# Both recurrence gates of 128 channels in the four quarters of the TensorE array, the second gate from a copy of its input with the halves exchanged

## The chip, the cores and the metric

The kernel runs on one core of one Trainium2 chip. The metric is the time of one execution on the device in microseconds (us); the number that counts is the median of a few runs. A profile is one further execution, recorded by the hardware profiler.

A core has five engines with a queue each: PE (TensorE: matmuls; the loads of their stationary operand are shown apart, as PEld), DVE (VectorE), ACT (ScalarE), POOL (GpSimd) and SP (SyncE, which in this kernel issues all DMA transfers). Each engine works through its queue in the order of the program; an instruction that has to wait holds up all that stand behind it.

## What is computed

Two layers over 256 context and 256 latent tokens of width 1024. Each layer is a half feed-forward block, a token mixer with four branches, and a second half feed-forward block. One of the four branches is a recurrence (RG-LRU) over 256 channels, in both directions; the change touches its two gates alone. Cut to them:

```
LRU_BLOCKS = 4                       # 256 channels in 4 blocks of 64
def rglru_coeffs(u, w_a, b_a, w_x, b_x, lam):
    ub = u.reshape(b, t, LRU_BLOCKS, w // LRU_BLOCKS)
    r = sigmoid(einsum('btnc,nce->btne', ub, w_a).reshape(b, t, w) + b_a)
    i = sigmoid(einsum('btnc,nce->btne', ub, w_x).reshape(b, t, w) + b_x)
    log_a = -LRU_C * r * softplus(-lam)
    return exp(log_a), sqrt(-expm1(2.0 * log_a)) * (i * u)
def rglru_mixer(...):
    u = dw_conv(xr, lru_conv_w, LRU_CONV_K // 2) + lru_conv_b
    for direction, reverse in ((0, False), (1, True)):
        a, b = rglru_coeffs(u, ...)
        h = linear_scan(a, b, h0, reverse)
```

So each gate multiplies every block of 64 channels by a 64x64 matrix of its own, for 512 tokens, and there are two gates, two directions, four blocks and two layers.

## The kernel before, in words

All activations lie with channels on partitions and tokens in columns. The large products (L196, three passes in a reduced format that stand for one full-precision product) make up nearly all of the kernel; their weights come in by DMA (L128), three buffers deep, and are split into a high and a low part by ACT (L150) and DVE (L151).

In the mixer, `self.recurrence` is a generator whose pieces are put between the large products by a clock of planned time (`later`, `spend`; a `yield n` asks for the next piece n planned nanoseconds later). A scheduler of the framework then sets the final order on each engine; that order is fixed before the run. Two attention branches are woven in by the same clock (`attend`): scores (L721, two heads at a time, each on 64 partitions), transposes of the probabilities (`turn`, L701, into the PSUM bank `C`), and values (L735, two heads at a time, each into 64 columns of the array). `heads` uses the bank `E` for small transposes (`flip`, L638). PSUM tiles have a tag each, with so many buffers: `A` 3, `B` 2, `C` 1, `D` 1, `E` 1.

The recurrence takes 128 channels (`c`, two of them) and a direction (`d`) at a time, so four steps in a layer and eight in the kernel. `U[c]` holds the 128 channels of its input for both halves of the tokens; it comes out of four DVE operations (`conv`, L569 and three of L575). For each gate `gate` runs two fp32 matmuls of 128x128 by 256 columns (L772) with a block-diagonal stationary operand `bd`: two 64x64 matrices on the diagonal, zeros beside them. Both write the bank `E`, and ACT takes it from there with a Tanh (L773). The second gate follows 1300 planned ns after the first. `bd` is loaded once for a layer.

An fp32 matmul stands in the trace as two records. Counts of "x4" and the like below are records.

Of the kernel before, what the change touches and what calls it, by code (L numbers as in the profile page):

```python
# [8 lines left out]
F32 = mybir.dt.float32  # L9
F32R = mybir.dt.float32r  # L10
AF = mybir.ActivationFunctionType
# [4 lines left out]
L = 2  # L16
# [19 lines left out]
class Net:  # L36
# [13 lines left out]
        self.n += 1  # L50
        return f"{s}{self.n}"

    BUFS = dict(b=12, nb=2, nr=2, ya=4, yp=4, m=8, a=6, l=5, r=3, t=2)
    BANKS = dict(A=3, B=2, C=1, D=1, E=1)

    def blk(self, tag, shape=(128, 512), dt=F32):
# [264 lines left out]

    def first_factors(self, n, s, R):
        nc = self.nc
        ms = self.small((64, 128), "ms", 2)
        nc.vector.tensor_scalar(ms, n["ps"][s], 1.0 / D, EPS, op0=ALU.mult, op1=ALU.add)
        pt = self.ps("A", (128, 2, 32))
        nc.tensor.transpose(pt[:].rearrange("p g n -> p (g n)"), ms, self.ident[:64, :64])
        v = self.small((128, 2), "v4")
        nc.vector.tensor_copy(v, pt[:, :, 0])
        for f in self.factors(n, s, v, R):  # L330
            f()
# [425 lines left out]
                T[b, 1] = self.turn(P.pop(b)[1], nk(b))  # L757
            yield 2 * step

    def recurrence(self, segs, out, U, bd, sp2, hb, step):  # L760
        nc = self.nc
        S3 = lambda x: x[:].rearrange("p (s t) -> p s t", s=2)
        for c in range(2):
            for d in range(2):
                k = 2 * d + c
                u = U[c] if d == 0 else U[c][:, ::-1, :]

                def gate(j, g):
                    pz = self.ps("E")
                    for s in range(2):  # L770
                        src = s if d == 0 else 1 - s
                        nc.tensor.matmul(pz[:, 256 * s:256 * s + 256], bd[:, 4 * j + k], U[c][:, src], start=True, stop=True)  # L772
                    nc.scalar.activation(g, pz, AF.Tanh, scale=0.5, bias=hb[:, 4 * j + k:4 * j + k + 1])  # L773

                t, q, b = (self.blk("r") for _ in range(3))
                gate(0, t)
                yield 1300
                gate(1, b)
                nc.scalar.activation(q, t, AF.Exp, scale=sp2[:, 4 + k:5 + k], bias=sp2[:, 4 + k:5 + k])
                nc.scalar.activation(t, t, AF.Tanh, scale=sp2[:, k:k + 1], bias=sp2[:, k:k + 1])  # L780
                nc.vector.scalar_tensor_tensor(S3(b), S3(b), 1.0, u, op0=ALU.add, op1=ALU.mult)
                yield step
                w = self.blk("t")
                nc.vector.tensor_scalar(q, q, 1.0, None, op0=ALU.add)
                nc.vector.scalar_tensor_tensor(w, t, 1.0, q, op0=ALU.add, op1=ALU.mult)
                nc.vector.scalar_tensor_tensor(q, w, 4.0, q, op0=ALU.subtract, op1=ALU.mult)
                nc.scalar.activation(t, t, AF.Sqrt)
                nc.vector.tensor_tensor(t, t, q, op=ALU.mult)
                nc.vector.tensor_scalar(q, q, -0.5, -1.0, op0=ALU.mult, op1=ALU.add)
                nc.vector.tensor_tensor(b, b, t, op=ALU.mult)  # L790
                h = self.blk("ya") if d == 0 else t
                w = slice(None) if d == 0 else slice(None, None, -1)
                nc.vector.tensor_tensor_scan(h[:, w], q[:, w], b[:, w], 0.0, op0=ALU.mult, op1=ALU.add)
                if d == 0:
                    f = h
                yield step
            for s in segs:
                w, w2 = slice(256 * s, 256 * s + 256), slice(256 * (1 - s), 256 * (1 - s) + 256)
                nc.vector.tensor_tensor(f[:, w], f[:, w], h[:, w2], op=ALU.add)
            out.append(f)  # L800

    def mixer(self, l, H, nxt):
# [4 lines left out]
        lo, hi = qr  # L807
        segs = self.segs(qr)
        ns = len(segs)
        bd = self.sp.tile([128, 8, 128], F32, name=self.nm("bd"), tag="bd", bufs=1)  # L810
        nc.sync.dma_start(bd, self.a["bd"][l])
        sp2, hb = self.softplus_terms(l)
        gq = self.head_gains(l)
# [8 lines left out]


        two = lambda: self.blk("b", (128, 2, 256))
        U, dk, dv = [two(), two()], [two(), two()], [two(), two()]
        wf, wt = self.take("fm", l, 0), self.take("tm", l, 0)
        F = [self.ps("A"), self.ps("A")]
# [14 lines left out]
        for c in range(2):  # L842
            t = self.blk("m", (128, 2, 256))
            nc.scalar.activation(t, F[c][:].rearrange("p (s t) -> p s t", s=2), AF.Copy)
            self.conv(U[c], t, lambda k: par[:, O_LW + 2 * k + c:O_LW + 2 * k + c + 1], [(0, 2), (-2, 0), (-1, 1), (1, 3)],
                      par[:, O_LB + c:O_LB + c + 1])

        gain = lambda j: gq[:, 64 * j:64 * j + 64]
        Y = [None, [], [], []]
        self.later(5000, lambda: self.job(self.recurrence(segs, Y[2], U, bd, sp2, hb, 5500 if full else 7000), (l, "lru")))  # L850
        dq = [two() if full else None, two()]
        self.tokens(l, 1, H, qr, lambda t, ps: self.heads(ps, t, 4, gain(2), dq, None, "m"))
        self.tokens(l, 2, H, ALL, lambda t, ps: nc.scalar.activation(dv[t // 2][:, t % 2], ps, AF.Copy))
# [160 lines left out]
def layout(x, c, ctx, c_ctx, w_mod, b_mod, norm_g, ffn_w_gate, ffn_w_up, ffn_w_down, w_in, b_gate, conv_a_w,  # L1014
           qk_norm_g, attn_sink, lru_conv_w, lru_conv_b, lru_w_a, lru_b_a, lru_w_x, lru_b_x, lru_lam, na_rel_bias,
           w_branch, w_out):
    A = {}
    t = np.concatenate([ctx[0], x[0]], axis=0)
    A["x"] = t.T.reshape(KC, 128, NT)
    A["c"] = np.stack([c_ctx, c[0]], axis=1).reshape(KC, 128, 2).transpose(1, 0, 2)  # L1020
    A["cst"] = constants()
    sets = []
    for i in range(3):
        sets += [[24 * i + 2 * s, 24 * i + 2 * s + 1, 24 * i + 8 + 2 * s, 24 * i + 9 + 2 * s] for s in range(4)]
        sets += [[24 * i + 16 + 4 * s + g for g in range(4)] for s in range(2)]
    sets = np.array(sets)
    wm = w_mod.reshape(L, 2, 4, 128, 72, 128)[:, :, :, :, sets]
    A["first"] = wm[0, :, :, :, :4].transpose(3, 0, 2, 1, 4, 5).reshape(4, 2, 128, 2048)
    A["mod"] = w_mod.reshape(L, D, 72, 128)[:, :, sets].transpose(0, 2, 3, 4, 1).reshape(L, 18, 2, 2, 128, D) \
        .transpose(0, 1, 2, 4, 3, 5).reshape(L, 18, 2, 128, 2048)  # L1030
    A["rows"] = np.broadcast_to(np.stack([c_ctx, c[0]]).reshape(1, 2, 2, 512), (128, 2, 2, 512))
    gu = np.stack([ffn_w_gate, ffn_w_up], axis=2).reshape(L, 2, 2, KC, 128, FT, 128)
    A["gu"] = gu.transpose(0, 1, 5, 4, 2, 3, 6).reshape(L, 2, FT, 128, 2048)
    dn = ffn_w_down.reshape(L, 2, 2, FH, 128, 8, 128)
    A["dn"] = dn.transpose(0, 1, 2, 5, 4, 3, 6).reshape(L, 2, 2, 8, 128, FH * 128)
    part = lambda n, w: w_in[:, :, COL[n]:COL[n] + w]
    fm = np.stack([part(n, 256) for n in FM], axis=1).reshape(L, 5, KC, 128, 2, 128)
    A["fm"] = fm.transpose(0, 1, 3, 4, 2, 5).reshape(L, 5, 128, 2048)
    tmw = np.stack([part(n, 256) for n in TM], axis=1)
    perm = np.concatenate([np.arange(64 * h, 64 * h + 64) for pr in HEADS for h in pr])  # L1040
    tmw[:, 4] = tmw[:, 4][:, :, perm]
    A["tm"] = tmw.reshape(L, 5, KC, 128, 256).transpose(0, 1, 3, 2, 4).reshape(L, 5, 128, 2048)
    gl = w_in[:, :, COL["gl"]:].reshape(L, KC, 128, 4, 8, 128).transpose(0, 3, 4, 2, 1, 5)
    wb = np.array(w_branch)
    wb[:, 1] = wb[:, 1][:, perm]
    wb = wb.reshape(L, 4, 2, 128, 8, 128).transpose(0, 1, 4, 3, 2, 5)
    A["gb"] = np.concatenate([gl, wb], axis=4).reshape(L, 4, 8, 128, 1280)
    wo = w_out.reshape(L, KC, 128, 4, 2, 128)
    A["wo"] = wo.transpose(0, 3, 2, 4, 1, 5).reshape(L, 4, 128, 2048)
    col = lambda v: v.reshape(L, -1, 128).transpose(0, 2, 1)  # L1050
    bm = b_mod.reshape(L, 72, 128)[:, sets.reshape(-1)]
    par = [col(norm_g), bm.transpose(0, 2, 1), col(b_gate), col(conv_a_w), col(lru_conv_w), col(lru_conv_b),
           col(lru_b_a), col(lru_b_x), col(lru_lam)]
    A["par"] = np.concatenate(par, axis=2)
    rep = np.concatenate([qk_norm_g.reshape(L, 256), attn_sink], axis=1)
    A["rep"] = np.broadcast_to(rep[:, None, :], (L, 128, 260))
    bd = np.zeros((L, 2, 2, 2, 2, 64, 2, 64), np.float32)
    for j, w in enumerate((lru_w_a, lru_w_x)):
        w = w.reshape(L, 2, 2, 2, 64, 64)
        for b in range(2):  # L1060
            bd[:, j, :, :, b, :, b, :] = w[:, :, :, b]
    A["bd"] = bd.reshape(L, 8, 128, 128).transpose(0, 2, 1, 3)
    A["nb"] = na_rel_bias[:, :, :, ::-1]
    return {k: np.ascontiguousarray(v) for k, v in A.items()}

# [23 lines left out]
```

## Time and profile before

| | |
|---|---|
| median of 3 runs | 2020.85 us (2020.05 to 2020.87) |
| time of the profiled execution | 2021.12 us |
| its span, first to last instruction | 2019.2 us |
| PE / PEld / DVE / ACT / POOL busy | 99% / 86% / 66% / 40% / 5% |
| granted TensorE clock | 1.000 (2.4 GHz) over the span |
| DMA | 295.50 MB, 146 GB/s on average |

Engine busy shares are averages over stages. The time of an execution is its span and about 2 us around it; the profiled execution is 0.27 us above the median. A piece of the chain of waits reads: start in us, length in us, what was done, and how many records it holds.

### The profile page before, as it was taken

To read this page: it belongs to the slowest core of one execution; us is meant where nothing else is said; L and a number is where in the kernel's file an instruction comes from. 1 tells how busy PE (TensorE), PEld (TensorE's weight loads), DVE (VectorE), ACT (ScalarE), POOL (GpSimd) and SP (SyncE) were. 2 spreads that over 40 slices of the span, in tenths; PEclk is the share of its full clock that TensorE was granted. 3 is DMA by queue.
4 is the path that set the end of the run, shared out by engine and by line. 5 is a ranking of instruction groups with operands and counts; after the bars stand their busy time and mean duration, and the time that the engine had idled before them with its cause. 6 is when DMAs were issued, how large, how long until landed. Compare 5 with 4: busy or idle time off the path is not lost.

```text
span 2019.2 us, 29778 instructions
## 1 busy us (share of the span) xinstructions
PE 1997.5 (99%) x11732; PEld 1732.6 (86%) x11732; DVE 1329.5 (66%) x2905; ACT 799.8 (40%) x1311; POOL 102.5 (5%) x105
## 2 busy tenths in 40 slices
PE   7999999999999999999999999999999999999999
PEld 5888887897797788988888898888888999999999
DVE  5869986677455545685733368689844788775554
ACT  4322222366334434332223233322323676664443
POOL 0000000220010000200000020000002101010000
PEclk9999999999999999999999999999999999999999
DMA  9645653522221234253522234446434224463553
GB/s 351 212 175 194 222 191 133 175 69 67 80 87 66 79 102 149 84 183 138 190 104 92 72 140 157 163 170 245 178 123 138 82 92 139 152 232 146 174 186 122
DMA packets 61548, 295.50 MB, mean 146 GB/s; under 512 B 14688, under 2 KB 16352, under 8 KB 38240
## 3 DMA queue, kind: packets, MB, share of 16 engines
q1 hardware_dynamic: 61408, 293.60, 41.7%
q8 instruction: 92, 1.51, 0.3%
q14 instruction: 48, 0.39, 0.1%
HBM read 292.53 MB, written 1.05 MB: 145 GB/s over the span
## 4 chain that ended last, share of the span: by engine, by line
PE 93%; DVE 3%; DMA 2%; issue 1%; ACT 1%; POOL 0%; SPq 0%; ACTq 0%; POOLq 0%; DVEq 0%
PE A L196 56%; PE B L196 32%; DVE a L256 1%; DMA b<-in_first 1%; PE B L721 1%; PE D L735 1%; PE C L701 1%; DVE wl L151 1%; PE E L772 1%; DMA w<-in_dn 0%; DMA par<-in_par 0%; PE E L638 0%; DMA yp<-in_first 0%; ACT wh L150 0%; DVE x L452 0%
## 5 line engine op out<-in xcount | busy, mean ns | idle before, releaser
L150 ACT ACTIVATE wh<-w 128x1024 fp32r<-128x1024 f32 (+2 forms) x476 | 428.2, 905 | 863.9 <-PE A L196 364.4
L196 PE MATMUL A<-h,wh 128*128 128x512 f32 (+1 forms) x2880 | 750.3, 348 | 1.3 <-DVE h L393 0.7
L151 DVE TENSOR_TENSOR wl<-w,wh 128x1024 fp32r<-128x1024 f32 (+2 forms) x476 | 490.3, 1033 | 287.4 <-ACT wh L150 284.8
L196 PEld LDWEIGHTS A<-h,wh 128*128 128x128 f32 x2880 | 496.6, 189 | 73.5 <-issue 10.9
L196 PE MATMUL A<-h,wl 128*128 128x512 f32 (+1 forms) x1440 | 494.9, 344 | 1.6 <-DVE wl L151 1.6
L196 PE MATMUL B<-h,wh 128*128 128x512 f32 (+1 forms) x1472 | 397.5, 355 | 0.0
L256 DVE CUSTOM_DVE_ANT_0 a<-w,rows 128x512 f32<-128x512 f32 x512 | 351.5, 697 | 35.8 <-DMA w<-in_mod 26.7
L196 PEld LDWEIGHTS A<-h,wl 128*128 128x128 f32 x1440 | 272.6, 189 | 35.3 <-DVE wl L151 2.9
L196 PEld LDWEIGHTS B<-h,wh 128*128 128x128 f32 x1472 | 261.8, 189 | 38.7
L196 PE MATMUL B<-h,wl 128*128 128x512 f32 (+1 forms) x736 | 261.1, 355 | 0.2 <-DVE wl L151 0.2
L196 PEld LDWEIGHTS B<-h,wl 128*128 128x128 f32 x736 | 139.1, 189 | 20.0 <-DVE wl L151 0.6
L354 POOL TENSOR_TENSOR nb<-nb,l 128x256 f32<-128x256 f32 x60 | 60.6, 1023 | 1360.2 <-ACT l L352 1360.2
L196 PE MATMUL A<-b,wh 128*128 128x512 f32 (+1 forms) x492 | 126.3, 346 | 1.8 <-ACT wh L150 1.8
L485 DVE TENSOR_TENSOR t<-t,B 128x512 f32<-128x512 f32 (+1 forms) x88 | 54.2, 618 | 106.5 <-PE B L196 105.5
L196 PE MATMUL B<-b,wh 128*128 128x512 f32 (+1 forms) x408 | 110.7, 358 | 0.0
L196 PEld LDWEIGHTS A<-b,wh 128*128 128x128 f32 x492 | 85.9, 189 | 13.9 <-ACT wh L150 2.7
L196 PE MATMUL A<-b,wl 128*128 128x512 f32 (+1 forms) x246 | 85.1, 346 | 0.8 <-DVE wl L151 0.8
L196 PE MATMUL A<-wh,h 128*128 128x256 f32 x448 | 84.9, 287 | 0.0
L196 PEld LDWEIGHTS B<-b,wh 128*128 128x128 f32 x408 | 72.8, 189 | 11.2
L196 PE MATMUL B<-b,wl 128*128 128x512 f32 (+1 forms) x204 | 73.1, 358 | 0.3 <-DVE wl L151 0.3
L196 PE MATMUL A<-m,wh 128*128 128x512 f32 (+1 forms) x280 | 72.8, 347 | 0.0
L196 PEld LDWEIGHTS A<-wh,h 128*128 128x128 f32 x448 | 71.0, 191 | 0.2
(237 smaller groups left out, 2255.0 us busy)
## 6 DMA issues: line engine op xcount, KB each, us to landing
w<-in_gu SPq DMA_DIRECT2D x88, 1024.0 KB, 4.9
w<-in_mod SPq DMA_DIRECT2D x64, 1024.0 KB, 4.8
w<-in_dn SPq DMA_DIRECT2D x64, 704.0 KB, 4.1
w<-in_gb SPq DMA_DIRECT2D x64, 640.0 KB, 3.8
w<-in_fm SPq DMA_DIRECT2D x10, 1024.0 KB, 4.8
w<-in_tm SPq DMA_DIRECT2D x10, 1024.0 KB, 5.2
w<-in_wo SPq DMA_DIRECT2D x8, 1024.0 KB, 4.8
b<-in_first SPq DMA_DIRECT2D x20, 256.0 KB, 6.2
```

The lines of the kernel that those rows point to most:

```text
L150: nc.scalar.activation(hi[i][:, :e], t[:, o:o + e], AF.Copy)
L151: nc.vector.tensor_tensor(lo[i][:, :e], t[:, o:o + e], hi[i][:, :e].bitcast(F32), op=ALU.subtract)
L196: mm = lambda *a, **k: self.pin(self.nc.tensor.matmul(*a, **k)) if self.pinned else self.nc.tensor.matmul(*a, **k)
L256: nc.vector.tensor_tensor_reduce(out=junk, in0=w[:, g, k], in1=self.rows[:, v, k], scale=1.0, scalar=0.0, op0=ALU.mult, op1=ALU.add, accum ...
L354: nc.gpsimd.tensor_tensor(n["acc"][s], n["acc"][s], sq, op=ALU.add)
L485: nc.vector.tensor_tensor(s[:, lo:hi], s[:, lo:hi], ps[1][:, lo:hi], op=ALU.mult)
L701: nc.tensor.transpose(pt[:, j], p[:, 128 * j:128 * j + 128], self.ident)
L721: nc.tensor.matmul(S[hh][:, 256 * j:256 * j + 256], queries(sg, j)[rows, pr, qw], keys(j, pr)[rows], start=True, stop=True)
L735: nc.tensor.matmul(y[64 * hh:64 * hh + 64, 128 * qb:128 * qb + 128], value(j, pr, hh), T[u, hh][:, j], start=(j == 0), stop=(j == n - 1), ...
L772: nc.tensor.matmul(pz[:, 256 * s:256 * s + 256], bd[:, 4 * j + k], U[c][:, src], start=True, stop=True)
```

## The change

Gate 1 (`j` = 0) now runs as two fp32 matmuls of 64x64 by 512 columns: rows 0 to 63 of the array into its columns 0 to 63, and rows 64 to 127 into columns 64 to 127, both into the bank `E`. Gate 2 (`j` = 1) runs in the other two quarters, from rows 0 to 63 into columns 64 to 127 and the reverse, into the bank `C`. So that its results land on the right partitions, it reads `V[c]`, a copy of `U[c]` with its two halves of 64 partitions exchanged. Two DMAs for each `c` make that copy, eight in the kernel, 128 KB each, issued from SP. The four matmuls are issued together; the `yield 1300` between the gates is gone. `bd` loses its zeros. The reversed order of token halves for `d` = 1 moves from the matmul to the Tanh that reads PSUM.

In the first layer's norm a small tile (`ms`) now comes from another ring of buffers (`l`).

```diff
-    BUFS = dict(b=12, nb=2, nr=2, ya=4, yp=4, m=8, a=6, l=5, r=3, t=2)
+    BUFS = dict(b=12, nb=2, nr=2, ya=4, yp=4, m=8, a=6, l=5, r=3, t=2, v=2)
...
-        ms = self.small((64, 128), "ms", 2)
+        ms = self.half()[0:64, 0:128]
...
-                def gate(j, g):
-                    pz = self.ps("E")
-                    for s in range(2):
-                        src = s if d == 0 else 1 - s
-                        nc.tensor.matmul(pz[:, 256 * s:256 * s + 256], bd[:, 4 * j + k], U[c][:, src], start=True, stop=True)
-                    nc.scalar.activation(g, pz, AF.Tanh, scale=0.5, bias=hb[:, 4 * j + k:4 * j + k + 1])
-
                 t, q, b = (self.blk("r") for _ in range(3))
-                gate(0, t)
-                yield 1300
-                gate(1, b)
+                pz = self.ps("E"), self.ps("C")
+                for j in range(2):
+                    for i in range(2):
+                        r, w = slice(64 * i, 64 * i + 64), slice(64 * (i ^ j), 64 * (i ^ j) + 64)
+                        nc.tensor.matmul(pz[j][w], bd[r, 4 * j + k], (U, V)[j][c][r].rearrange("p s t -> p (s t)"),
+                                         start=True, stop=True, tile_position=(64 * i, 64 * (i ^ j)))
+                for g, p, j in ((t, pz[0], 0), (b, pz[1], 1)):
+                    p = S3(p) if d == 0 else S3(p)[:, ::-1, :]
+                    nc.scalar.activation(S3(g), p, AF.Tanh, scale=0.5, bias=hb[:, 4 * j + k:4 * j + k + 1])
...
-        bd = self.sp.tile([128, 8, 128], F32, name=self.nm("bd"), tag="bd", bufs=1)
+        bd = self.sp.tile([128, 8, 64], F32, name=self.nm("bd"), tag="bd", bufs=1)
...
+        V = [self.blk("v", (128, 2, 256)) for _ in range(2)]
...
+            for i in range(2):
+                nc.sync.dma_start(V[c][64 * i:64 * i + 64], U[c][64 - 64 * i:128 - 64 * i])
...
-        for b in range(2):
-            bd[:, j, :, :, b, :, b, :] = w[:, :, :, b]
-    A["bd"] = bd.reshape(L, 8, 128, 128).transpose(0, 2, 1, 3)
+        bd[:, j] = w if j == 0 else w[:, :, :, ::-1]
+    A["bd"] = bd.reshape(L, 8, 128, 64).transpose(0, 2, 1, 3)
```

What the change does to the fixed order shows at three places. A letter with a number is a PSUM or SBUF tile, `x2` two matmuls in a row; L775 is the new line of the gates.

First place: PE at the first step of the recurrence in layer 0, before the change. `b_3351` is `U[0]`.

```order
L196 MATMUL A_3713<-wh_3362,h_309 128x256
L772 MATMUL E_3743<-b_3351,bd_3310 128x256 x2
L196 MATMUL A_3756<-wh_3361,h_294 128x256
...
L196 MATMUL A_3756<-wh_3362,h_303 128x256
L772 MATMUL E_3774<-b_3351,bd_3310 128x256 x2
L196 MATMUL A_3756<-wh_3362,h_304 128x256
...
L638 MATMUL E_3784<-cst,m_3637 128x128 x2
```

Behind the change (`b_3353` is `U[0]`, `v_3351` is `V[0]`):

```order
L196 MATMUL A_3719<-wh_3364,h_309 128x256
L775 MATMUL E_3749<-b_3353,bd_3310 64x512 x2
L196 MATMUL A_3769<-wh_3363,h_294 128x256
...
L196 MATMUL A_3769<-wh_3364,h_302 128x256
L775 MATMUL C_3750<-v_3351,bd_3310 64x512
L196 MATMUL A_3769<-wl_3366,h_302 128x256
L196 MATMUL A_3769<-wh_3364,h_303 128x256
L638 MATMUL E_3787<-cst,m_3639 128x128 x2
...
L196 MATMUL A_3769<-wh_3364,h_305 128x256
L775 MATMUL C_3750<-v_3351,bd_3310 64x512
L638 MATMUL E_3794<-cst,m_3648 128x128 x2
```

The gate-1 pair stands where the first gate stood, but the two matmuls of gate 2 come apart: the first 13 rows of L196 later, the second five rows of L196 behind that, with two small transposes among them; each stands alone between products over the whole array. Layer 1 has the same order at its first step. In the other six steps the four stand together, as in the second place.

The copies on SP at this place (`w` rows are weight transfers, which wait for a buffer to come free; `b_3354` and `v_3352` are `U[1]` and `V[1]`):

```order
L128 DMA w_3853<-in_fm 128x2048
L850 DMA v_3351<-b_3353 64x512 x2
L850 DMA v_3352<-b_3354 64x512 x2
L128 DMA w_4049<-in_fm 128x2048
L128 DMA w_4169<-in_gb 128x1280
```

The copies stand behind the two weight transfers that were next in the queue, and the weight transfers that follow stand behind the copies.

Second place: PE at the third step of layer 0, where the near attention runs. Before:

```order
L196 MATMUL A_4162<-h_298,wl_4047 128x512
L772 MATMUL E_4200<-b_3352,bd_3310 128x256 x2
L196 MATMUL A_4162<-h_300,wh_4045 128x512
...
L701 MATMUL C_4210<-cst,a_4095 128x128 x2
L196 MATMUL A_4162<-h_304,wh_4045 128x512
...
L772 MATMUL E_4218<-b_3352,bd_3310 128x256 x2
L196 MATMUL A_4162<-h_306,wh_4045 128x512
```

Behind the change:

```order
L196 MATMUL A_4060<-h_300,wl_3858 128x512
L775 MATMUL E_4132<-b_3354,bd_3310 64x512 x2
L775 MATMUL C_4133<-v_3352,bd_3310 64x512 x2
L196 MATMUL A_4060<-h_302,wh_3856 128x512
...
L196 MATMUL A_4060<-h_304,wh_3856 128x512
L701 MATMUL C_4146<-cst,a_4044 128x128 x2
```

A transpose of the attention into the bank `C` (L701) now comes four rows of L196 behind a gate that fills the same bank. This happens in three more steps: eight rows of 512 columns behind it in step 4 of layer 0, eight and seven rows of 256 columns in steps 2 and 3 of layer 1. The queue of ACT at this place (L779 is the new line of the Tanhs; `a_4149` is taken from `C` behind the L701 above):

```order
L687 ACTIVATE a_4109,mx_4106<-B_4102,mx_4106 128x256
L687 ACTIVATE a_4113,mx_4106<-B_4103,mx_4106 128x256
L779 ACTIVATE r_4129<-E_4132,lr_3343 128x512
L779 ACTIVATE r_4131<-C_4133,lr_3343 128x512
L780 ACTIVATE r_4130<-r_4129,lr_3339 128x512
L703 ACTIVATE a_4149<-C_4146 128x256
```

The Tanh that empties `C` stands second behind the Tanh of gate 1; in step 4 of layer 0 two L687 of 512 columns stand between the two, and in step 2 of layer 1 a copy out of `A`.

Third place: PE at the values of the near attention in layer 1. Before:

```order
L196 MATMUL A_13592<-h_10031,wl_13515 128x256
L735 MATMUL D_13690<-a_13569,b_12911 64x128
L735 MATMUL D_13690<-a_13667,b_12911 64x128
L735 MATMUL D_13690<-a_13569,b_12911 64x128
...
L735 MATMUL D_13690<-a_13667,b_12912 64x128
L196 MATMUL A_13719<-h_10017,wh_13583 128x256
```

Behind the change:

```order
L196 MATMUL A_13618<-h_10037,wl_13527 128x256
L735 MATMUL D_13702<-a_13595,b_12919 64x128
L196 MATMUL A_13731<-h_10023,wh_13609 128x256
...
L196 MATMUL A_13731<-h_10028,wh_13609 128x256
L735 MATMUL D_13702<-a_13679,b_12919 64x128
L735 MATMUL D_13702<-a_13595,b_12919 64x128
...
L735 MATMUL D_13702<-a_13679,b_12920 64x128
L196 MATMUL A_13731<-h_10027,wl_13611 128x256
```

One L735 of the eight now runs alone, eight rows of L196 ahead of the other seven. There are five such places (two in layer 0, one of them 1 and 3 in place of 4; three in layer 1). In both layers all other groups of L721 and L735 keep their size.

## Rows read from the trace of the kernel before

**Rows 1.** The page: span, busy time, and the chain by engine.

```profile
span 2019.2 us, 29778 instructions
PE 1997.5 (99%) x11732; PEld 1732.6 (86%) x11732; DVE 1329.5 (66%) x2905; ACT 799.8 (40%) x1311; POOL 102.5 (5%) x105
PE 93%; DVE 3%; DMA 2%; issue 1%; ACT 1%; POOL 0%; SPq 0%; ACTq 0%; POOLq 0%; DVEq 0%
```

**Rows 2.** The gates' line: records, ns least/median/most, first and last start.

```profile
L772 PE MATMUL E<-b,bd x64: 377/378/484, 428.7 to 1669.4; 128*128 128x256 f32 x64
```

**Rows 3.** The chain in the mixer of layer 0: start us, us, what.

```profile
428.83 0.86 PE E L772 x4
429.69 1.78 PE A L196 x15
...
470.14 1.39 PE A L196 x6
```

**Rows 4.** The same chain where attention packs the array, and behind it.

```profile
458.34 0.63 PE B L721 x4
...
463.55 0.59 PE D L735 x8
464.14 1.58 PE A L196 x6
...
467.31 1.06 PE B L721 x8
468.38 0.90 PE A L196 x3
...
485.31 1.02 PE D L735 x16
```

**Rows 5.** L273 alone in one us (stretch, length, busy, records); a transpose in the chain.

```profile
28.87:29.87 1.00, 1.00 (x47) 1.00 (x42) 1.00 1.04 401
```

```profile
509.23 0.22 PE C L701 x2
```

**Rows 6.** Timeline of PE: the first gate of layer 0 and of layer 1.

```profile
428.67 1.02 PE L772 MATMUL E<-b,bd 128*128 128x256 f32 x4
...
1593.29 1.02 PE L772 MATMUL E<-b,bd 128*128 128x256 f32 x4
```

**Rows 7.** Timeline of DVE and SP: end of U[0], the weight transfer, both layers.

```profile
427.13 0.75 DVE L575 SCALAR_TENSOR_TENSOR b<-m,par,b 128x510 f32<-128x510 f32 x1
...
1591.75 0.74 DVE L575 SCALAR_TENSOR_TENSOR b<-m,par,b 128x510 f32<-128x510 f32 x1
...
427.25 0.33 SPq L128 DMA_DIRECT2D w<-in_fm  x1
...
1591.86 0.33 SPq L128 DMA_DIRECT2D w<-in_fm  x1
```

**Rows 8.** DMA issues: count, KB each, median us from issue to landing.

```profile
w<-in_fm SPq DMA_DIRECT2D x10, 1024.0 KB, 4.8
...
nr<-in_nb SPq DMA_DIRECT2D x32, 64.0 KB, 7.1
...
out_dram<-x SPq DMA_DIRECT2D x8, 128.0 KB, 1.7
```

**Rows 9.** Timeline of ACT: a copy, a gate's Tanh, two exponentials.

```profile
428.87 0.38 ACT L624 ACTIVATE m<-A 128x256 f32<-128x256 f32 x1 [2.05 <-PE A L196]
429.73 0.69 ACT L773 ACTIVATE r<-E,lr 128x512 f32<-128x512 f32 x1
...
470.19 0.69 ACT L687 ACTIVATE a<-B,mx 128x512 f32<-128x512 f32 x1 [2.84 <-DVE mx L685]
470.86 0.68 ACT L687 ACTIVATE a<-B,mx 128x512 f32<-128x512 f32 x1
```

**Rows 10.** Waits of PE in layer 0 (us, times, longest); a late gate of layer 1.

```profile
PE E L638 <- DVE m L646: 0.6, 1, 0.6
...
1646.14 1.13 PE E L772 x4
```

More of the change, by code (lines that the diff above doesn't have):

```diff
@@ L758, in attend, with recurrence @@
             yield 2 * step
-    def recurrence(self, segs, out, U, bd, sp2, hb, step):
+    def recurrence(self, segs, out, U, V, bd, sp2, hb, step):
         nc = self.nc
@@ L846, in mixer @@
                       par[:, O_LB + c:O_LB + c + 1])
+            for i in range(2):
+                nc.sync.dma_start(V[c][64 * i:64 * i + 64], U[c][64 - 64 * i:128 - 64 * i])
         gain = lambda j: gq[:, 64 * j:64 * j + 64]
         Y = [None, [], [], []]
-        self.later(5000, lambda: self.job(self.recurrence(segs, Y[2], U, bd, sp2, hb, 5500 if full else 7000), (l, "lru")))
+        self.later(5000, lambda: self.job(self.recurrence(segs, Y[2], U, V, bd, sp2, hb, 5500 if full else 7000), (l, "lru")))
         dq = [two() if full else None, two()]
@@ L1056, in layout @@
     A["rep"] = np.broadcast_to(rep[:, None, :], (L, 128, 260))
-    bd = np.zeros((L, 2, 2, 2, 2, 64, 2, 64), np.float32)
+    bd = np.zeros((L, 2, 2, 2, 2, 64, 64), np.float32)
     for j, w in enumerate((lru_w_a, lru_w_x)):
         w = w.reshape(L, 2, 2, 2, 64, 64)
-        for b in range(2):
-            bd[:, j, :, :, b, :, b, :] = w[:, :, :, b]
-    A["bd"] = bd.reshape(L, 8, 128, 128).transpose(0, 2, 1, 3)
+        bd[:, j] = w if j == 0 else w[:, :, :, ::-1]
+    A["bd"] = bd.reshape(L, 8, 128, 64).transpose(0, 2, 1, 3)
     A["nb"] = na_rel_bias[:, :, :, ::-1]
```

## The prediction

> **What bounds the kernel now.** I read the page first: PE is busy for 99% of the span and 93% of the chain that ended last is PE [rows 1]. So what counts is PE's own time, and every place where PE is made to wait; ACT at 40% and DVE at 66% matter only where PE waits for them. The gates' line is small: 64 records between 428.7 and 1669.4 us, in the two mixers [rows 2]. The chain gives what four of them, one gate, cost: 0.86 us, and the L196 rows behind run at their usual pace (15 of 256 columns in 1.78 us, 0.12 each) [rows 3]. So a step of the recurrence, two gates, costs PE 2 x 0.86 = 1.72 us, and all eight steps 13.8 us. No more than that can be had.
>
> **What a packed group costs.** The kernel already packs the array in two ways, and the chain shows the price. L721 puts two matmuls on the two halves of the rows: 4 records take 0.63 us and 8 take 1.06, so 4 records more cost 0.43, what two records of 256 columns cost in L772 (0.86 / 2): the pair does run side by side. What is left, 0.63 - 0.43 = 0.20, is paid once in a group. L735 puts two on the halves of the columns: 8 records 0.59, 16 records 1.02, again 0.43 for 8, and 0.16 once. Behind each group the next L196 rows are late: 3 of them take 0.90 and 6 take 1.58 [rows 4], where 6 take 1.39 behind an unpacked group [rows 3]; that is 0.19 to 0.20 more. So going into a packed group and out again costs 0.16 + 0.20 = 0.36 us with 64 columns and 0.40 with 128. L772 pays neither.
>
> **Six steps with four quarters together.** The trace has no matmul of 64 by 64. The nearest rows are L735 (two at once) and L273 of the first stage, which puts four on quarters of the columns: 47 records in 1.00 us [rows 5], where records of the same 128 columns take 0.11 each one by one, in L701. So four at once run at full rate. Bounds: all four side by side, two rounds (the two records of an fp32 matmul) of 512 columns, 2 x 0.43 = 0.86 us and 0.36 around it, 1.22 us; all one behind another, 4 x 0.86 + 0.36 = 3.80. I take the first, since both kinds of packing reach it on their own. That is 1.22 - 1.72 = -0.50 a step, **-3.0 us** for six.
>
> **Two steps that come apart.** At the first step of each layer the order has the gate-1 pair, then the matmuls of gate 2 singly between L196 rows. A lone quarter takes as long as four: three groups of 1.22 = 3.66 against 1.72, +1.94 a step, **+3.9 us**.
>
> **The copies.** PE waits for the first copy at the lone matmul. `U[0]` is ready at 427.13 + 0.75 = 427.9 us, but the copy is issued behind the weight transfer of 427.25 [rows 7], which lands 4.8 us later, at 432.05. 128 KB alone take 1.7 us [rows 8]; 896 KB more take 3.1, so 128 KB behind it about 0.4, an estimate: landing at 432.5. PE starts the pair at 428.67 [rows 6], is through at 429.9 and has 13 rows of 0.12 left: it is there at 431.45, and waits 1.0 us. In layer 1 the pair starts at 1593.29 [rows 6], the transfer at 1591.86 [rows 7]: it lands at 1596.66, the copy at 1597.1, PE is there at 1596.07, again 1.0. **+2.0 us**. Bounds: if the copy overtakes the weights it lands at 427.9 + 1.7 = 429.6 and PE never waits, 0; if it fares like `nr` (7.1 us, several at once) [rows 8] it lands at 435.0, 3.5 each, 7. I take the transfers as they are issued, one behind another. The other copies and the second half are there before PE asks. On SP the copies wait until `U[1]` is through at about 431; the weights behind them were issued at 440 and 1598 before, later than that, so they lose nothing.
>
> **The bank `C`.** `C` has one buffer, and the near attention transposes into it. In four steps an L701 stands a few L196 rows behind the gates, and waits until the second Tanh has emptied the bank. A Tanh starts 0.04 us after the last record (428.67 + 1.02 = 429.69, and 429.73) and takes 0.69 [rows 6, 9], so two take 1.42. PE comes out of the group (0.20) and works through its rows in that time; a wake-up of PE costs about as much as the way out, so the wait is about 1.42 less the rows. Step 3 of layer 0: 4 rows of 0.232 (1.39 / 6 [rows 3]), 0.5 us. Step 4 of layer 0: two exponentials of 0.68 stand between the Tanhs [rows 9], 2.8 less 8 rows (1.86), 0.9. Step 2 of layer 1: a copy of about 0.35 [rows 9] between, 1.77 less 8 rows of 0.12 (0.96), 0.8. Step 3 of layer 1: 1.42 less 7 rows (0.84), 0.6. **+2.8 us**; bounds 0 (if the Tanh of gate 1 can run while gate 2 is still in the array) and twice as much, about 5, if ACT is late.
>
> **Values torn apart.** Five groups of L735 lose one matmul to a place of its own: that one costs its two records alone, 2 x 0.11, and the way in and out, 0.36, and the other seven (or three) take as many rounds as eight (four). 5 x 0.57 = **+2.9 us**. Each is fixed by the order and packed as L735 is now; I see no bound below 5 x 0.36 = 1.8.
>
> **Waits that go.** In layer 1 a gate waited for the bank `E` (1.13 us for the four records against 0.86); two banks end that. In layer 0 a transpose in `E` waited 0.6 us for DVE [rows 10]; PE now comes there some 3 us later, ACT too, and I expect the wait to go. **-0.9 us**, or 0 if ACT is later than PE.
>
> **What I cost at nothing.** The Tanh reads PSUM in another order with the same count of elements, 0.69 us as before; should ACT pay for the order, it would lengthen the wait at `C` alone. `bd` shrinks by half and its load still ends long before the first gate; it could cost PE only if it came after 428 us. The `ms` tile lies in the first stage, where the order on PE is unchanged and a buffer of the ring that is late would show as a wait of DVE. The copies are 1 MB of 295, and the DMA engines have room beside them; uncovered they would be the 1.0 us waits above, which are counted.
>
> Sum: -3.0 + 3.9 + 2.0 + 2.8 + 2.9 - 0.9 = +7.7 us, against the profiled execution 2021.12 + 7.7 = 2028.8. That execution is 0.27 above the median, so the median should be **2028.5 us**.
>
> **The rivals.**
>
> *A bank takes from one half of the rows at a time.* The two matmuls of gate 1 come from different halves of the rows and write one bank, `E`. L721 gives each half of the rows a bank of its own, and L735 and L273 share a bank with all rows each, so no row here shows this case. Then, in the order of the queue, the eight records need five rounds (one alone, then pairs across the banks, one alone): 2.15 + 0.36 = 2.51, +0.79 a step, +4.7 for six in place of -3.0; the gate-1 pairs of the first steps take 2.08 in place of 1.22, +1.7 for two; the Tanh of gate 1 starts a round earlier, -1.7. 7.7 + 7.7 + 1.7 - 1.7 = +15.4: **2036 us**. The Trainium skill states this rule (TensorEngine Tiling (Array Packing), Gotcha 1: PSUM Pressure): different row tiles write to different banks and cannot access the same one at once. No run here shows whether it holds for halves that also write different partitions; by the rule as worded the sum would be +15.4 us, by the rows of L721 and L735 taken together +7.7. Chance 0.11.
>
> *Two quarters at a time.* Rows and columns both shared may allow only a diagonal pair: four rounds, 2.08, +0.36 a step for six (+2.2 in place of -3.0), with the first Tanh hidden, -2.5: +10.4, **2031 us**. Against it: each kind of sharing alone runs at full rate. Chance 0.08. One at a time (3.80): about 2043, chance 0.02.
>
> *Copies early and `C` free in time.* Without those two terms, +2.9: **2023.5 us**, inside what counts as no change. For it: the scheduler put the L701 where it expected no wait; against it: the durations above. Chance 0.14.
>
> *Faster.* The quarters leave most of the array idle in the first steps and between groups; if the L196 products beside them ran on in that time, the twelve groups of gates (six of four and two times three, 14.6 us) would cost nothing, and the sum would be 7.7 - 14.6 = -6.9: **2014 us**. It decides from 11.7 of the 14.6 us hidden. Against it: no L196 row ran beside L721 or L735, both pay for going in and out. Chance 0.05.
>
> **How the numbers follow.** My forecast has 0.60. A measurement of this kernel tells about 0.2%, 4 us, from no change. Slower by more: forecast, bank, two or one at a time, 0.81; within: 0.14; faster: 0.05. The likeliest case alone lies between 2025 and 2032 (copies and `C` between half and one and a half of their terms). The range takes in the early copies below and the bank above, 2022.5 to 2036.5; outside stay the faster case, one at a time, and the edges.
>
> **What would show it.** Right: eight records of the gates within 1.1 us in six steps, starting in fours; 0.36 us lost around each; at 431 and 1596 us a PE wait that ends with a DMA into `v`; PE waits of 0.5 to 0.9 us at L701 that end with the gates' Tanh; five more groups of L735, each of two records. Wrong: record starts in pairs 0.43 apart (two at a time) or five rounds (bank); no wait for `v`. The weakest terms are the landing of the copies and the state of ACT when the gates end.

## The result and the profile after

The median went from 2020.85 us (2020.05 to 2021.17, 5 runs) to 2036.45 us (2035.60 to 2040.43, 5 runs): a ratio of 1.0082 (1.0072 to 1.0093), +15.6 us. The change makes the kernel slower, as forecast, but by twice the 7.7 us of the forecast. It is the very time that the rival of the bank gave, and that is chance: the trace refutes that rival (below). The profiled execution after took 2035.60 us, 14.5 more than that of before.

The page, in the lines of [rows 1]:

```profile
span 2033.7 us, 29793 instructions
PE 2007.0 (99%) x11732; PEld 1728.4 (85%) x11732; DVE 1330.8 (65%) x2905; ACT 799.5 (39%) x1311; POOL 102.6 (5%) x105
PE 91%; DVE 4%; DMA 3%; ACT 1%; issue 1%; POOL 0%; SPq 0%; ACTq 0%; POOLq 0%; DVEq 0%
```

PE is still busy for 99%, so a busy share shows nothing here. In the chain 2% went from PE to DVE and DMA.

**Where the time went.** The same weight split of ACT (L150), once ahead of and once behind a mixer, shows how far the two traces lie apart. The timeline of ACT at layer 0, before and then after:

```profile
393.71 1.06 ACT L150 ACTIVATE wh<-w 128x1024 fp32r<-128x1024 f32 x1 [1.18 <-PE A L196]
515.78 0.75 ACT L150 ACTIVATE wh<-w 128x640 fp32r<-128x640 f32 x1
```

```profile
391.90 1.06 ACT L150 ACTIVATE wh<-w 128x1024 fp32r<-128x1024 f32 x1 [1.18 <-PE A L196]
522.02 0.75 ACT L150 ACTIVATE wh<-w 128x640 fp32r<-128x640 f32 x1
```

From the first row to the second, layer 0's mixer, 122.07 us became 130.12, +8.05. At layer 1 the same two splits stand at 1558.33 and 1724.22 before and at 1564.63 and 1738.67 after: 165.89 us became 174.04, +8.15. Between them the distance stays (6.24 and 6.30). The 1.8 us by which after is ahead at 391.90 belong to what comes before, which differs from one execution to the next: in the traces of the experiments the same row starts between 392.4 and 394.7. So all of the loss of this execution, 16.2 us, lies in the two mixers, in equal parts; the forecast had 3.85 in each.

**The four quarters.** The timeline of PE at the second step of layer 0 (start us, us from first start to last end, x records):

```profile
449.96 0.28 PE L196 MATMUL A<-wh,h 128*128 128x256 f32 x1
450.17 0.65 PE L775 MATMUL E<-b,bd 64*64 64x512 f32 x2
450.18 0.65 PE L775 MATMUL C<-v,bd 64*64 64x512 f32 x2
450.64 0.60 PE L775 MATMUL E<-b,bd 64*64 64x512 f32 x2
450.66 0.59 PE L775 MATMUL C<-v,bd 64*64 64x512 f32 x2
451.18 0.39 PE L196 MATMUL A<-wh,h 128*128 128x256 f32 x1
451.41 0.28 PE L196 MATMUL A<-wl,h 128*128 128x256 f32 x1
```

Four records start within 0.02 us, the other four 0.48 us later: two rounds. So four run side by side, also the two of gate 1, which come from different halves of the rows and write one bank, `E`. From the L196 at 449.96 to the one at 451.41 are 1.45 us; less the 0.24 of two L196, the group costs 1.21, forecast 1.22, and 0.5 less than the two gates of before [rows 3].

**The first step.** The chain in layer 0, and in layer 1:

```profile
426.10 5.77 DMA v<-b
...
431.91 1.43 PE C L775 x2
433.34 0.73 PE A L196 x2
...
434.50 0.64 PE A L196 x3
435.14 1.90 PE C L775 x2
...
1598.84 6.35 DMA v<-b
...
1605.23 1.07 PE C L775 x2
```

and the waits of PE over the whole execution (us, times, longest):

```profile
PE C L775 <- DMA v<-b: 4.9, 2, 2.7
PE C L701 <- ACT r L779: 1.7, 4, 0.6
```

The copy lands 5.77 and 6.35 us after its issue, and PE waits for it 4.9 us in all, not 2.0. What follows was not in the forecast at all: the second lone matmul takes 1.90 us (two records) and three L196 rows 0.64, where three took 0.36 before (0.12 each [rows 3]). The windows of the stretch show why (length, then busy time and count of PE, PEld, DVE, ACT, POOL, then the granted clock as a share of 2.4 GHz, DMA share, GB/s):

```profile
429.60:431.90 2.30, 0.19 (x2) 0.00 (x0) 1.35 (x4) 0.00 (x0) 0.71 (x2) 1.00 0.88 241
432.00:438.80 6.80, 6.80 (x20) 3.79 (x21) 1.54 (x3) 2.09 (x3) 0.55 (x1) 0.54 0.02 6
438.80:445.00 6.20, 6.20 (x52) 6.20 (x52) 3.18 (x7) 5.61 (x12) 1.01 (x1) 0.96 0.00 0
...
1606.20:1613.00 6.80, 6.80 (x26) 4.93 (x26) 1.97 (x4) 3.69 (x6) 0.12 (x1) 0.54 0.33 135
```

PE stands still for most of the first window, to 431.91 in the chain; then the granted clock is at its lower level, 1.2 GHz, for most of the next 6.8 us, and back at 2.4 GHz behind that. The same happens behind the wait of layer 1, and not in this execution alone: over the span, the granted clock is 0.995 to 0.997 in all five executions of the changed kernel, against 0.998 to 1.000 in the run below in which PE does not wait (e8). In the second window PE counts as fully busy, with 20 records in 6.8 us, where the next has 52 in 6.2. Before, the clock was 1.00 in both mixers, and the longest wait of PE in them was this:

```profile
PE C L701 <- DVE a L694: 0.9, 1, 0.9
```

**The bank `C` and the torn values.** The chain in layer 0 at steps 3 and 4 and behind:

```profile
466.83 0.58 PE E L775 x2
...
467.90 1.25 ACT r L779 x2
...
469.20 0.44 PE C L701 x2
...
480.95 0.36 PE D L735 x2
...
489.13 1.44 ACT a L687 x4
490.57 0.59 ACT r L779
...
491.20 0.66 PE C L701 x4
...
493.47 0.36 PE D L735 x2
```

Here PE gives way to ACT, as forecast: L701 waits until both Tanhs are through, in step 4 with the L687 between them. PE loses 0.45 and 0.87 us at these two (the ends of the records around them, less the rows' own time), 0.70 and 0.55 in layer 1: 2.6 in all, forecast 2.8. A torn value takes 0.36 and the way out behind it, 0.20: 0.56, forecast 0.57.

### The profile page after: what moved, and what is told of

Read it like the earlier page. It is cut to its first block, busy times and chain, and to the rows that moved or that the text cites. A ratio compares the mean times of both kernels' runs of the same rounds, so it can differ in the third digit from the quotient of the medians.

```text
span 2033.7 us, 29793 instructions
## 1 busy us (share of the span) xinstructions
PE 2007.0 (99%) x11732; PEld 1728.4 (85%) x11732; DVE 1330.8 (65%) x2905; ACT 799.5 (39%) x1311; POOL 102.6 (5%) x105
## 4 chain that ended last, share of the span: by engine, by line
PE 91%; DVE 4%; DMA 3%; ACT 1%; issue 1%; POOL 0%; SPq 0%; ACTq 0%; POOLq 0%; DVEq 0%
PE A L196 55%; PE B L196 32%; DVE a L256 1%; PE D L735 1%; DMA b<-in_first 1%; DVE wl L151 1%; PE B L721 1%; PE C L701 1%; DMA v<-b 1%; DMA w<-in_dn 0%; PE E L638 0%; ACT wh L150 0%; PE C L775 0%; PE E L775 0%; DMA par<-in_par 0%
## 5 line engine op out<-in xcount | busy, mean ns | idle before, releaser
L150 ACT ACTIVATE wh<-w 128x1024 fp32r<-128x1024 f32 (+2 forms) x476 | 428.2, 906 | 865.1 <-PE A L196 357.7
L196 PE MATMUL A<-h,wh 128*128 128x512 f32 (+1 forms) x2880 | 750.0, 347 | 1.1 <-ACT h L392 0.5
L196 PEld LDWEIGHTS A<-h,wh 128*128 128x128 f32 x2880 | 496.7, 189 | 77.7 <-issue 15.3
L196 PE MATMUL A<-h,wl 128*128 128x512 f32 (+1 forms) x1440 | 495.5, 344 | 1.6 <-DVE wl L151 1.6
L196 PE MATMUL B<-h,wh 128*128 128x512 f32 (+1 forms) x1472 | 397.7, 355 | 0.0
L196 PEld LDWEIGHTS A<-h,wl 128*128 128x128 f32 x1440 | 272.8, 189 | 35.3 <-DVE wl L151 2.9
L196 PEld LDWEIGHTS B<-h,wh 128*128 128x128 f32 x1472 | 261.9, 189 | 38.7
L196 PE MATMUL B<-h,wl 128*128 128x512 f32 (+1 forms) x736 | 261.1, 355 | 0.2 <-DVE wl L151 0.2
L196 PEld LDWEIGHTS B<-h,wl 128*128 128x128 f32 x736 | 139.2, 189 | 20.0 <-DVE wl L151 0.6
L196 PE MATMUL A<-b,wh 128*128 128x512 f32 (+1 forms) x492 | 126.4, 346 | 1.4 <-ACT wh L150 1.4
L196 PE MATMUL B<-b,wh 128*128 128x512 f32 (+1 forms) x408 | 110.8, 358 | 0.0
L196 PEld LDWEIGHTS A<-b,wh 128*128 128x128 f32 x492 | 85.9, 190 | 13.4 <-ACT wh L150 2.2
L196 PE MATMUL A<-wh,h 128*128 128x256 f32 x448 | 87.8, 293 | 0.0
L196 PE MATMUL A<-b,wl 128*128 128x512 f32 (+1 forms) x246 | 85.2, 346 | 0.6 <-DVE wl L151 0.6
L196 PEld LDWEIGHTS B<-b,wh 128*128 128x128 f32 x408 | 72.8, 189 | 11.2
L196 PEld LDWEIGHTS A<-wh,h 128*128 128x128 f32 x448 | 73.9, 199 | 2.5 <-ACT l L626 0.8
L196 PE MATMUL B<-b,wl 128*128 128x512 f32 (+1 forms) x204 | 73.2, 359 | 0.3 <-DVE wl L151 0.3
L196 PE MATMUL A<-m,wh 128*128 128x512 f32 (+1 forms) x280 | 72.8, 348 | 0.0
```

The costliest lines, as they stand in the source:

```text
L150: nc.scalar.activation(hi[i][:, :e], t[:, o:o + e], AF.Copy)
L196: mm = lambda *a, **k: self.pin(self.nc.tensor.matmul(*a, **k)) if self.pinned else self.nc.tensor.matmul(*a, **k)
```

## The experiments

Theory A, formed on this trace: the excess is the wait for the copy, longer than forecast, and the lower clock behind it. Theory B: the four quarters, the transfers or the new order cost PE more in themselves.

**e1_no_copy.** The second gate reads `U` where it read `V`, so it computes with the wrong half of the channels; there are no transfers, and the scheduler keeps four together in all eight steps.

```diff
-                        nc.tensor.matmul(pz[j][w], bd[r, 4 * j + k], (U, V)[j][c][r].rearrange("p s t -> p (s t)"),
+                        nc.tensor.matmul(pz[j][w], bd[r, 4 * j + k], U[c][r].rearrange("p s t -> p (s t)"),
...
-            for i in range(2):
-                nc.sync.dma_start(V[c][64 * i:64 * i + 64], U[c][64 - 64 * i:128 - 64 * i])
```

> Gate 2 reads U itself: the copy V and its DMAs are left out (so the second gate works on the wrong half of the channels); the four quarters, the two banks and the missing yield stay as in the changed kernel, and all eight steps now issue their four matmuls together. Theory A (the loss is PE's wait for the copies at the first step of each layer, the lone quarters around it, and the half clock that follows the wait): no wait on a DMA into v, granted clock 1.000, what is left is 8 x -0.5 for the gates, +2.6 for the waits at bank C, +2.9 for the values torn apart, -0.9 for waits that go: 2020 to 2022 us. Theory B (the four-quarter groups themselves bring the clock down or hold up what follows): 2028 us or more, and a clock below 1.000.

2022.94 us, ratio 1.0012 (1.0002 to 1.0022), clock 1.000 in the profiled execution. That is 0.9 above A's range and 5 below B's: A's case, with a miss in its size. By the same L150 rows the mixers cost +1.2 and +0.8 us in place of +8.05 and +8.15. The quarters, the bank `C` and the torn values together are thus worth +2 us; 14.2 of 16.2 hang on the copy: the waits for it, the two steps that come apart, and the clock. A's terms gave +0.6 for this run; it counted the waits at L638 as gone, and here they are 1.5 us.

**e2_warm_wait.** Twenty matmuls without use on PE, between the gate-1 pair and the gate-2 pair at the first step of each layer; all else is the changed kernel, but the gate-2 pair stays together.

```diff
+                        if k == 0 and j == 1 and i == 0:
+                            self.warm(20, "D")
```

> The changed kernel, with 20 dummy matmuls of 128 columns (0.218 us each, 4.4 us) pinned between gate 1 and gate 2 at the first step of each layer, so that PE works through the wait for the copy; gate 2 then runs as a pair. Theory A (the clock falls because PE stands idle for 2 to 3 us): clock 1.000; the first steps cost 1.22 + 4.4 + 1.22 = 6.8 us where four together cost 1.22, +5.6 each, so about 11 us over the kernel without copies, 2031 to 2032 us, 4 to 6 us under the changed kernel although its wait is filled with more work than the wait was long. Theory B (the clock falls because quarters fill the array too little): clock still 0.997 in both places, 2036 us or more.

2032.33 us, ratio 1.0059 (1.0044 to 1.0074): though PE does more work, 4.1 us less than the changed kernel, as A said (0.3 above its range). The timeline of PE at the first step of layer 0, and the windows over the places of the wait:

```profile
427.68 1.07 PE L777 MATMUL E<-b,bd 64*64 64x512 f32 x4
428.68 4.73 PE L310 MATMUL D<-cst 128*128 128x128 f32 x40
433.35 1.08 PE L777 MATMUL C<-v,bd 64*64 64x512 f32 x4
```

```profile
430.00:439.00 9.00, 9.00 (x74) 8.05 (x73) 4.00 (x9) 4.44 (x8) 1.68 (x2) 1.00 0.26 80
1602.00:1611.00 9.00, 9.00 (x73) 8.04 (x72) 4.83 (x10) 6.11 (x9) 1.01 (x1) 1.00 0.42 139
```

The clock stays at 2.4 GHz. So it is PE's standing still that brings the lower clock, and not the transfers or the gates' quarters as such. Gate 2's lone matmuls of the first step are a pair here; that they don't bring it either, e9 shows (below). The twenty matmuls hold PE for 433.35 - 428.68 = 4.67 us, longer than the wait that they replace, so the clock's part is more than the 4.1 (below).

**e3_copies_only** and **e4_ms_only.** The kernel before with the transfers alone, into a tile that nobody reads; and with the `ms` edit alone.

```diff
+            for i in range(2):
+                nc.sync.dma_start(V[64 * i:64 * i + 64], U[c][64 - 64 * i:128 - 64 * i])
...
-        ms = self.small((64, 128), "ms", 2)
+        ms = self.half()[0:64, 0:128]
```

> The kernel before, with the eight copies of U added on SP (into one buffer that nothing reads; the small tile of the first norm comes from ring l as in the changed kernel, to make room). Theory A (the copies cost only where PE waits for them): no PE wait more than before, 2019 to 2021 us. Rival (the copies hold up the weight transfers around them): 2 to 4 us more than the kernel before, with PE waits on wh or wl after 430 and 1600 us.

> The kernel before with the first norm's small tile from ring l, nothing else. The profile of the changed kernel was 1.2 to 2.2 us ahead of the one before from 100 us on until the first mixer. If that is the edit: 2019 to 2019.8 us. If it is the run: 2020.85 us, no change.

2021.11 us, ratio 1.0003 (0.9994 to 1.0013), and 2020.88 us, 1.0001 (0.9992 to 1.0011). Neither costs anything that shows: these transfers matter only when PE waits for them. (e3 lies 0.1 above its range, far from its rival.)

**e9_act_queue.** Why the copy is late: its transfers go out from ScalarE's queue, where no weights stand ahead of them.

```diff
-                nc.sync.dma_start(V[c][64 * i:64 * i + 64], U[c][64 - 64 * i:128 - 64 * i])
+                nc.scalar.dma_start(V[c][64 * i:64 * i + 64], U[c][64 - 64 * i:128 - 64 * i])
```

> The changed kernel with its transfers into V issued from ScalarE's queue in place of SyncE's, behind no weight transfer of that queue; the scheduler then keeps the four quarters together in all eight steps. Theory Q (the copy is late because SyncE's queue has the weights ahead of it): the first copy lands 1.7 to 2.5 us after its issue, PE waits under 1 us for it, clock 1.0 in the mixers: 2022.5 to 2025 us. Theory E (the copy is late because the DMA engines are busy with the weights, whatever queue it is in): it lands 5 to 6 us after its issue as in the changed kernel, PE waits 2 us or more with the half clock behind: 2029 us or more.

2035.56 us, ratio 1.0072 (1.0058 to 1.0086). The chain in layer 0:

```profile
426.92 5.53 DMA v<-b
...
432.49 2.44 PE C L775 x4
```

its wait of PE, and its windows behind the two waits:

```profile
PE C L775 <- DMA v<-b: 7.6, 2, 3.9
```

```profile
432.50:439.00 6.50, 6.50 (x29) 4.69 (x30) 1.78 (x5) 3.99 (x6) 0.07 (x1) 0.61 0.04 10
1604.50:1611.00 6.50, 6.50 (x33) 4.65 (x34) 1.89 (x5) 4.04 (x7) 0.00 (x0) 0.74 0.04 9
```

The copy is hardly earlier from the other queue: 5.53 us, against 1.7 for a store of 128 KB [rows 8]. With four together PE asks for it sooner and waits 3.7 us in layer 0 and 3.9 in layer 1, with the lower clock around and behind it again, though no gate matmul stands alone here. Theory Q falls: it is not SyncE's order that holds the copy back. That it shares the DMA engines with the 1 MB in flight fits their busy share, 0.88 during the wait of the changed kernel and 0.02 behind it; no run has such a copy with the engines free, so what it takes by itself is not shown. The Trainium skill (DMA: Bandwidth & Descriptors, section "Issuing engines are not separate DMA queues") says that transfers run on the same 16 DMA engines and interleave, whichever engine started them; by that rule next to nothing is won by another queue, and this run agrees: 5.53 us from ScalarE's queue, 5.77 from SyncE's.

**e8_copies_early.** The changed kernel, with the recurrence begun 7000 planned ns later, so that the copies have landed when PE comes.

```diff
-        self.later(5000, lambda: self.job(self.recurrence(...
+        self.later(12000, lambda: self.job(self.recurrence(...
```

> The changed kernel with its transfers, but the recurrence begins 7000 later in the order, so that the copies have landed when the first step comes. Theory A (wait and half clock at the first step are the excess): no PE wait that ends with a transfer into V, clock 1.0 in both mixers, 2020 to 2023 us, three values torn. Theory B (the transfers disturb PE or the order in some other way): above 2028 us.

2021.60 us, ratio 1.0004 (0.9995 to 1.0013): one number in the code takes back 14.85 of the 15.6 us. The windows over the first steps:

```profile
424.00:445.00 21.00, 21.00 (x173) 19.85 (x172) 15.36 (x31) 13.46 (x25) 4.45 (x4) 1.00 0.38 127
1585.00:1610.00 25.00, 24.86 (x201) 23.03 (x200) 17.09 (x33) 15.17 (x25) 2.62 (x3) 1.00 0.39 131
```

PE has next to no gap (0.14 us in the two windows) and the full clock, though the transfers into `V` take 5.1 us in the median, no less than the 4.9 of the changed kernel. A holds. Its gain of eight packed steps does not show, though; e10 and e11 take that up.

**e5_vector_copy**, **e6_values_whole**, **e7_gate2_first.** The copy made by DVE, 0.42 us for each 64 by 512; then with a pause that keeps the values together; then with gate 2's Tanh first and a longer pause.

```diff
-                nc.sync.dma_start(V[c][64 * i:64 * i + 64], U[c][64 - 64 * i:128 - 64 * i])
+                nc.vector.tensor_copy(V[c][64 * i:64 * i + 64], U[c][64 - 64 * i:128 - 64 * i])
...
+                yield 1300        # e6; 2600 in e7
...
-                for g, p, j in ((t, pz[0], 0), (b, pz[1], 1)):
+                for g, p, j in ((b, pz[1], 1), (t, pz[0], 0)):        # e7
```

> V is written by VectorE copies (two per channel block, from one half of the partitions to the other) in place of the transfers; the result is the reference's and the order on PE is that of the run without a copy (eight groups of four, five values torn apart). Theory A (the change's cost over the run without a copy is the lone wait for the transfer and the half clock behind it): no wait for a transfer, granted clock 1.0 in both mixers, 2022.5 to 2025 us. Theory B (the second gate's matmuls, now from a true copy, cost PE more in themselves, or any wait for the copy brings the half clock): 2028 us or more.

> As the run with VectorE copies, with one pause of 1300 in the order behind the gates' Tanhs, so that the values' groups of L735 stay whole; one step of layer 1 then comes apart into single quarters. Theory A (a torn value costs 0.57 us each, five of them 2.9 us; a step that comes apart costs 1.9): 1.0 us below the run with VectorE copies, about 2022. Theory B (torn values cost nothing that the groups' way in and out doesn't give back elsewhere): 1.5 to 2 us above it.

> As the run with VectorE copies, with the Tanh of the second gate ahead of that of the first, so that bank C is empty one Tanh (0.7 us) earlier, and a pause of 2600 behind both in the order: one value torn in place of five, and the near attention's transposes farther behind the gates. By A's terms: eight steps of four together -0.5 each = -4.0, one torn value +0.6, waits at C under 0.5 in all, entries that were waits in E -0.9: 2017 to 2019 us, below the kernel before. By B (the gain of four side by side is used up elsewhere, since PE's other work sets the time): 2020.5 to 2022.

e5: 2025.42 us, ratio 1.0022 (1.0014 to 1.0031), 0.4 above A's range and 2.6 below B's, with the clock at 1.000 and no wait for a transfer: A's case. It is 2.5 us above e1. Of these 1.3 are longer waits of PE at L638 (2.8 us, 1.5 in e1), a transpose in the near attention's path whose input comes from DVE, on which the copies now stand as well; for the other 1.2 no row here shows a cause. The two longest:

```profile
PE E L638 <- DVE ss L629: 1.1, 1, 1.1
PE E L638 <- DVE m L646: 1.1, 1, 1.1
```

e6: 2027.47 us, ratio 1.0036 (1.0023 to 1.0048), 2.05 above e5, where A had 1.0 below it and B 1.5 to 2 above. e7: 2024.24, 1.0018 (1.0009 to 1.0027), outside both (A to 2019, B to 2022). Both are misses. In e6 and in e7:

```profile
PE E L638 <- DVE m L646: 4.1, 2, 3.3
```

```profile
PE E L638 <- DVE m L646: 4.6, 3, 2.8
```

The pauses moved the order on DVE as well, and in layer 0 PE stands still for 3.3 us in e6 and 2.8 in e7. Behind these waits, which have nothing to do with a transfer or a quarter, the clock falls too. The windows, e6 and then e7:

```profile
450.00:453.00 3.00, 2.90 (x14) 2.94 (x14) 0.00 (x0) 0.67 (x2) 0.00 (x0) 0.50 0.39 164
```

```profile
448.00:451.00 3.00, 3.00 (x16) 3.00 (x16) 0.00 (x0) 0.42 (x2) 0.00 (x0) 0.50 0.11 44
```

So B's number in e6 does not bear out B: the wait and the clock hide what the values bring. What a whole group of values is worth, e6 was to tell and does not; that term rests on the trace alone.

**e10_later_still**, **e11_later_pause.** Two tries for a version below both kernels: the transfers, a late recurrence, gate 2's Tanh first.

```diff
-        self.later(5000, ...
+        self.later(15000, ...        # e10; 12000 in e11
...
-                for g, p, j in ((t, pz[0], 0), (b, pz[1], 1)):
+                for g, p, j in ((b, pz[1], 1), (t, pz[0], 0)):
...
+                yield 1300        # e11
```

> The changed kernel with its transfers, the recurrence begun 10000 later in the order (3000 later than in the run with the copies early) and the Tanh of the second gate first: four quarters together in all eight steps, two values torn, bank C empty one Tanh earlier. By A's terms: -4.0 for the eight steps, +1.1 for the values, waits at C under 1 in all, -0.9 for E: 2017 to 2019 us. By B (what the steps save is taken back by waits for ACT and DVE in the near attention): 2020.5 to 2023.

> As the run with the copies early, with the Tanh of the second gate first and a pause of 1300 behind the gates: three values torn, the transposes into C behind the second gate farther away or free at once. By A's terms -4.0 + 1.7 - 0.9 and under 1 at C: 2017.5 to 2019.5 us. By B (waits for ACT and DVE take it back): 2020.5 to 2023.

2021.58 us, ratio 1.0002 (0.9993 to 1.0011), and 2022.23, 1.0003 (0.9994 to 1.0012): the numbers of B as it stands in these two, by which waits for ACT and DVE take the gain back. The 4 us of the eight steps seem to be used up by torn values and by small waits; that they add up to 4 us is not shown. The three longest of e10 in layer 1's mixer:

```profile
PE C L701 <- ACT r L779: 0.9, 1, 0.9
PE A L196 <- DVE t L945: 0.7, 1, 0.7
PE C L701 <- ACT wh L150: 0.5, 1, 0.5
```

No version run here beats the kernel before.

## Why the prediction was right in direction and half the size

Step by step, in its own order:

- **Packed groups, six steps at -0.50**: right. Four side by side in two rounds, 0.14 on the way in and 0.21 out (means over the groups of e1). The rivals of the bank, of two and of one at a time fall by the record starts. The rule of the Trainium skill on banks (TensorEngine Tiling (Array Packing), Gotcha 1: PSUM Pressure), on which the bank rival leaned, does not hold for this case: both row halves wrote bank `E` at once, with starts within 0.02 us, into different halves of its partitions. The faster rival falls too: no L196 record starts between the first and the last start of a group.
- **Two steps that come apart, +3.9**: they come apart as the order said, three groups each; the lower clock stretches the last two.
- **The copies, +2.0**: this step failed, twice. First in size: 4.9 us measured. The estimate let the weights land 4.8 us after their issue and the copy 0.4 later. In the trace the weights ahead land after 5.8 and 5.5 us and the copy 0.65 and 1.5 us behind them; e9 shows that the picture of one behind another, which I chose, does not hold: from a queue without weights the copy is as late. The 1.7 us from which the estimate took its price were a store's, not a copy's. Second, and worth more, the term had only the wait in it and not what the wait does to PE's clock. The forecast read the clock of the kernel before, 1.000, as a constant, although the change puts standstills of 2.1 and 2.7 us into a PE whose gaps in the mixers were near 1 us at most. The second error hangs on the first: at the forecast's own wait of 1.0 us the clock might well have stayed, as it did behind the two waits of 1.1 us in e5.
- **The clock**, not in the sum, costs some 6 us. By the windows: 6.8 us at 0.54 are 3.1 us less array time in each layer, 6.3. By the starts of the records, from the end of the wait until the pace is back: 7.57 us in layer 0 (431.91 to 439.48) and 8.38 in layer 1 (1605.23 to 1613.61), for two groups, one transpose (two records) behind each, and 15 and 22 rows of 256 columns, which at full clock are 2.44 + 0.44 + 1.80 = 4.68 and 5.52: 5.8 together. By the runs: the mixers of after lie 2.43 and 2.46 above those of e2 (by the L150 rows); the twenty matmuls of e2 add 4.67 each, after has the waits (4.9 in all) and one group more in each layer (1.22): 4.9 + 9.3 - 4.9 - 2.4 = 6.9; less 0.5, since the two groups and the twenty matmuls of e2 together take 6.86 us (in layer 0 from the L196 at 427.47 to the one at 434.57, less two rows) and not 4.67 + 2.44: 6.4.
- **The bank `C`, +2.8, and the torn values, +2.9**: 2.6 and 2.8 (five at 0.56), right.
- **Waits that go, -0.9**: the long gate of layer 1 is gone, and of the wait at L638 0.2 of 0.6 us is left. It is not a gain that the change brings by itself: in e1, where PE comes sooner, 1.5 us of such waits are back.
- **Costed at nothing**: the transfers and `ms`, shown by e3 and e4. That holds only while nobody waits.

With the two corrections the sum is 7.7 + 2.9 + (5.8 to 6.4) = 16.4 to 17.0; the mixers show 16.2, the medians 15.6. What lies between, 0.2 to 1.4 us, is not settled.

The rival "copies early and `C` free" named the right lever: e8 is that case for the copies, at 2021.6 us, where it said 2023.5. The two are not quite the same case: in e8 three values are torn in place of five, and L701 still waits 0.9 us for the Tanh.

## What to carry to other kernels

Cost a new wait of a busy PE twice: the wait itself, and the stretch at 1.2 GHz that may follow; here 4.9 us of waiting cost some 6 us more. A copy that PE needed at once did not overtake the weight transfer in flight by going out from another queue; what helped was to begin the consumer later (e8). When packing saves half a microsecond a step, count what it displaces (a shared bank, groups torn apart) before the gain: here the 4 us that the groups win did not show in the time of any run, with the wait repaired (e8, e10, e11).

## What the runs showed of the hardware

- Two 64x64 matmuls from different halves of the rows wrote different partitions of one PSUM bank at once: four starts within 0.02 us, the next four 0.48 us later.
- Behind standstills of 2.1 and 2.7 us, PE ran with the granted clock at the lower level for most of 6.8 us, in both layers; with standstills of 3.7 and 3.9 us (e9), 3.3 (e6) and 2.8 (e7) the clock fell as well, for about half as long in e6, e7 and the second of e9. With matmuls in the gap it did not (e2), nor behind single waits of 1.1 us (e5). In between it is not settled by the length alone: near 347 us, ahead of the first mixer, all 13 traces have two waits close together, 1.8 us in all, and the clock falls behind them in five (e2, e6, e7, e9, e11) and not in the other eight.
- The first 128 KB copy landed 5.5 to 6.4 us after its issue behind 1 MB of weights, from either of two queues; a store of that size takes 1.7 [rows 8].
- VectorE moved 64 partitions by 512 to the other half of the partitions in 0.42 us (e5).
